# RWKV chunk inverses: holding only the two heads' 64x64 diagonal blocks, and multiplying within them

## The chip, the core and the metric

One Trainium2 chip, of which the kernel uses one core. The metric is the device time of one execution in microseconds, the median of several runs. The core's engines work side by side, each through its own list of instructions in order: TensorE (PE in the profile, with its weight loads as PEld) multiplies matrices into PSUM, VectorE (DVE) and ScalarE (ACT) work elementwise and copy out of PSUM, GpSimd (POOL) works elementwise from SBUF, and SyncE (SP) issues the transfers. SBUF and PSUM have 128 partitions, the rows of a tile. A product `mm(out, lhsT, rhs)` loads lhsT as the weights and streams the columns of rhs past them; its form in the profile is rows\*columns of the weights, then what is streamed. "128\*64 128x64" is a product over 128 partitions with 64 output rows and 64 streamed columns. Each float32 product of this kernel appears as two instructions.

## The reference

Two layers of a hybrid backbone over 1024 latent and 256 context tokens with 1024 features, ending in an RMS norm. The first layer runs RWKV-7 time mixing beside Mamba-2, the second mLSTM beside attention. The part in question is the RWKV-7 scan, 8 heads of 64 features, in both directions of time:

```python
def step(S, inp):
    r_t, k_t, v_t, w_t, a_t, kk_t = inp
    Skk = jnp.einsum('dbhvk,dbhk->dbhv', S, kk_t)
    S = S * w_t[..., None, :] - Skk[..., :, None] * (kk_t * a_t)[..., None, :] + v_t[..., :, None] * k_t[..., None, :]
    return S, jnp.einsum('dbhvk,dbhk->dbhv', S, r_t)

xs = (dir_stack(r), dir_split(k_dir), dir_stack(v), dir_split(decay), dir_split(a), dir_stack(kk))
S_fin, y = lax.scan(step, S0, xs)
```

The kernel does not scan token by token. It takes 64 tokens at a time; within such a chunk the dependence of each token on the earlier ones is a triangular 64x64 system, and its inverse is applied to the whole chunk at once.

## The kernel before

The whole first layer but RWKV comes first, then a stage with RWKV alone and part of the first layer's output product (`oa` in the profile) between, then the rest. The RWKV stage works on pairs of heads: partitions 0 to 63 belong to one head, 64 to 127 to the other (`H[0]`, `H[1]`). Four such pairs (`ct`) go as two streams (`st` 0 and 1), each over two pairs one after the other. For each pair there are ten units (`gi`) of `NG` = 2 chunks in each direction, so `NJ` = 4 chunks of 64 tokens for each head. `lockstep` advances the two streams in turn; within a stream `pace` advances the next unit (`rwkv_unit`, which needs no state) beside the chain of the present one (`rwkv_chain`, which carries the state). 20 units a stream, 40 in all. The framework's scheduler then orders the instructions of each engine from this; in this stage no order is fixed by hand.

`rwkv_unit` computes decays and products elementwise on DVE and ACT (`P`, `E2`, `sg`, `AR`, `KB`), multiplies KB with AR on TensorE (64 rows, 128 columns) and masks the result into `MN`. From it it forms `MT`, the identity less the strictly triangular part, for each of the 4 chunks. Then `TT` becomes the transposed inverse by doubling: it starts from `MT` masked to pairs of tokens (`m1`), and for block sizes b = 2, 4, 8, 16, 32 (a level each)

- `px` = MT times Tm on TensorE, masked by DVE into `Xs` (L769);
- `pz` = TT times Xs, copied by ACT into the next `Tm` (L775), not at the last level;
- `pt` = Xs times TT, copied by ACT back into `TT` (L779).

PSUM tiles of these are `rec` (two buffers a stream, `rec0` and `rec1`). `MT` and `TT` hold, for each chunk, a 128x128 matrix with the two heads' 64x64 blocks on the diagonal and zeros elsewhere, put there once by a memset at the start; `Tm` and `Xs` hold the two heads' 64x64 blocks one above the other. `halves` issues for each chunk a product for the one head and one for the other, each over all 128 rows with 64 output columns; the zeros take the other head's rows out.

`rwkv_chain` runs for each chunk, both directions at a time, through PSUM tiles `ch`: `pw` = MN times the state and values `SV`; `pu` = TT times w (`ch<-w,TT`); the next state `pS` from SV, the identity (`mk`) and `KT`; the output `py` from MN, RZ and SV. All of its products have 128 rows and 64 columns.

Of the kernel before, what the change touches and what calls it, by code (L numbers as in the profile page):

```python
# [8 lines left out]
F32 = mybir.dt.float32  # L9
# [15 lines left out]
NG = 2  # L25
# [22 lines left out]
def _masks():  # L48
    parts = []
    o = 0  # L50

    def put(name, a):
        nonlocal o
        a = np.asarray(a, np.float32).reshape(128, -1)
        _MK[name] = (o, a.shape[1])
        parts.append(a)
        o += a.shape[1]

    put("id", np.eye(128))
    put("ones", np.ones((128, 128)))  # L60
    r = np.arange(128)
    hh = (r[:, None] // 64 == r[None, :] // 64)
    put("bd1", hh)
    put("triu", r[:, None] <= r[None, :])
    put("slt", r[:, None] < r[None, :])
    for d in range(2):
        ok = (r[:, None] <= r[None, :]) if d == 0 else (r[:, None] >= r[None, :])
        put(f"mb{d}", np.where(ok, 0.0, -1e30))
    put("end", np.zeros((128, 0)))
    i = r % 64  # L70
    mp, m1, lv = [], [], {b: [] for b in (1, 2, 4, 8, 16, 32)}
    for d in range(2):
        bef = (i[:, None] < np.arange(64)[None]) if d == 0 else (i[:, None] > np.arange(64)[None])
        inc = bef | (i[:, None] == np.arange(64)[None])
        beffull = (i[:, None] < i[None, :]) if d == 0 else (i[:, None] > i[None, :])
        mp += [np.concatenate([bef, inc], 1)] * NG
        m1.append((hh & beffull & (i[:, None] // 2 == i[None] // 2)) | np.eye(128, dtype=bool))
        for b in lv:
            c = np.arange(64)[None]
            lv[b].append(~inc & (i[:, None] // (2 * b) == c // (2 * b)) & (i[:, None] // b != c // b) | (i[:, None] == c))  # L80
    put("mP", np.concatenate(mp, 1))
    put("m1", np.concatenate(m1, 1))
    put("id2", i[:, None] == np.arange(64)[None])
    for b in lv:
        put(f"l{b}", np.concatenate(lv[b], 1))
    return np.ascontiguousarray(np.concatenate(parts, 1))
# [64 lines left out]
class K:  # L151
# [401 lines left out]
    def rwkv_setup(s, rp):  # L553
        nc = s.nc
        s.rp = rp
        s.mk2 = rp.tile([128, MASKS.shape[1] - NMK], F32, name="mk2")
        s.load(s.mk2, s.I["masks"][:, NMK:])
        s.w2 = rp.tile([128, 512], F32, name="w2")
        s.a2 = rp.tile([128, 512], F32, name="a2")
        s.load(s.w2, s.I["w2"])  # L560
        s.load(s.a2, s.I["a2"])
        s.smask = rp.tile([128, 2, NG, 64], F32, name="smask")
        nc.vector.memset(s.smask, 1.0)
        for d in range(2):
            nc.vector.memset(s.smask[:, d, :, 63 * d:63 * d + 1], 0.0)
        s.rc = rp.tile([128, 28], F32, name="rc")
        nc.vector.tensor_scalar_mul(s.rc[:, 0:16], s.p("w0", 0, 16), 0.5)
        ka = s.p("k_a", 0, 4)
        nc.vector.tensor_scalar_mul(s.rc[:, 16:20], ka, 0.5)
        nc.vector.tensor_scalar(s.rc[:, 20:24], ka, -0.5, 1.0, ALU.mult, ALU.add)  # L570
        nc.vector.tensor_scalar(s.rc[:, 24:28], ka, -1.0, 2.0, ALU.mult, ALU.add)
        s.tt, s.wa, s.rz, s.mt = {}, {}, {}, {}
        for st in range(2):
            for i in range(2):
                s.tt[st, i] = rp.tile([128, 2 * NG, 128], F32, name=f"TT{st}{i}")
                s.wa[st, i] = rp.tile([128, 2, 2, 64 * NG], F32, name=f"wa{st}{i}")
                s.rz[st, i] = rp.tile([128, 2 * NG, 2, 64], F32, name=f"RZ{st}{i}")
                nc.gpsimd.memset(s.tt[st, i], 0.0)
                nc.gpsimd.memset(s.wa[st, i], 0.0)
                nc.gpsimd.memset(s.rz[st, i], 0.0)  # L580
            s.mt[st] = rp.tile([128, 2 * NG, 128], F32, name=f"MT{st}")
            nc.gpsimd.memset(s.mt[st], 0.0)
        s.RX = {}
        s.tn = [0, 0]
        s.kk_d = [s.dram("kkd", (128, NT)) for _ in range(4)]
        s.bv_d = [s.dram("bvd", (128, NT)) for _ in range(4)]
        s.vt_d = [s.dram("vtd", (128, 20, 64)) for _ in range(4)]
# [60 lines left out]
    def rwkv_unit(s, st, ct, gi):  # L648

        nc, rp = s.nc, s.rp  # L650
# [6 lines left out]
        H = [slice(0, 64), slice(64, 128)]  # L657
# [81 lines left out]

        ident = s.m("id")  # L740
        for h in range(2):
            nc.vector.scalar_tensor_tensor(MT[H[h], :, H[h]], MN[H[h], :, 0, h], -1.0,
                                           ident[H[h], H[h]].unsqueeze(1).to_broadcast([64, NJ, 64]), ALU.mult, ALU.add)
        KT = tl("KT", [2, 64], 2)
        pk = [rec(64) for h in range(2)]
# [13 lines left out]

        Tm = tl("Tm", [64], 2)  # L760
        px = rec(64)
        halves(lambda j, Q: s.mm(px[Q, j], MT[:, j, Q], s.m("id2")))
        nc.vector.tensor_mul(dj(Tm), dj(px), bj("l1"))  # L763
        yield
        for b in (2, 4, 8, 16, 32):
            px = rec(64)
            halves(lambda j, Q: s.mm(px[Q, j], MT[:, j, Q], Tm[:, j]))
            Xs = tl("Xs", [64])
            nc.vector.tensor_mul(dj(Xs), dj(px), bj(f"l{b}"))  # L769
            yield  # L770
            if b < 32:
                pz = rec(64)
                halves(lambda j, Q: s.mm(pz[Q, j], TT[:, j, Q], Xs[:, j]))
                Tm = tl("Tm", [64], 2)
                nc.scalar.copy(Tm, pz)  # L775
            pt = rec(64)
            halves(lambda j, Q: s.mm(pt[Q, j], Xs[:, j], TT[:, j, Q]))
            for h in range(2):
                nc.scalar.copy(TT[H[h], :, H[h]], pt[H[h]])  # L779
            yield  # L780
        X["u", gi] = {"E2": E2, "MN": MN, "KT": KT, "SV": SV, "TT": TT, "RZ": RZ}

    def rwkv_chain(s, st, ct, gi):
        nc, rp = s.nc, s.rp
        X = s.RX[ct]
        H = [slice(0, 64), slice(64, 128)]
        U = X["u", gi]
        SV, TT, MN, KT, E2, RZ = (U[k] for k in ("SV", "TT", "MN", "KT", "E2", "RZ"))
        if gi == 0:
            X["y"] = rp.tile([128, 2, 20, 64], F32, tag=f"y{st}", name=s.name("y"))  # L790
        J = [(n, 2 * NG - 1 - n) for n in range(NG)]

        def both(t, n):
            return t[:, J[n][0]:J[n][1] + 1:J[n][1] - J[n][0]]

        if gi == 0:
            for h in range(2):
                nc.vector.memset(both(SV, 0)[H[h], :, 0, h], 0.0)

        def ch():  # L800
            return s.psum(f"ch{st}", (128, 2, 64))

        E = E2.rearrange("p j l -> p (j l)")
        ident = s.m("id")
        for n in range(NG):
            js = J[n]
            pw = ch()
            for d, j in enumerate(js):
                for h in range(2):
                    s.mm(pw[H[h], d], MN[:, j, 0, h], SV[:, j, 0, h])  # L810
            w = rp.tile([128, 2, 64], F32, tag=f"w{st}", name=s.name("w"))
            nc.scalar.mul(w, pw, -1.0)
            yield
            pu = ch()
            for d, j in enumerate(js):
                for h in range(2):
                    s.mm(pu[H[h], d], TT[:, j, H[h]], w[:, d])
            nc.vector.tensor_copy(both(SV, n)[H[0], :, 1, 0], pu[H[0]])
            nc.scalar.copy(both(SV, n)[H[1], :, 1, 1], pu[H[1]])
            yield  # L820
            if not (gi == s.NU - 1 and n == NG - 1):
                pS = ch()
                for d, j in enumerate(js):
                    for h in range(2):
                        s.mm(pS[H[h], d], ident[:, H[h]], SV[:, j, 0, h], True, False)
                    for h in range(2):
                        s.mm(pS[H[h], d], KT[:, j, h], SV[:, j, 1, h], False, True)
                nx = SV if n < NG - 1 else X["sv", gi + 1]
                e0 = 64 * js[0] + 63
                e1 = 64 * js[1]  # L830
                PL = E[:, e0:e1 + 1:e1 - e0].unsqueeze(2).to_broadcast([128, 2, 64])
                for h in range(2):
                    nc.vector.tensor_mul(both(nx, (n + 1) % NG)[H[h], :, 0, h], pS[H[h]], PL[H[h]])
                yield
            py = ch()
            for d, j in enumerate(js):
                for h in range(2):
                    s.mm(py[H[h], d], MN[:, j, 1, h], SV[:, j, 1, h], True, False)
                for h in range(2):
                    s.mm(py[H[h], d], RZ[:, j, h], SV[:, j, 0, h], False, True)  # L840
            nc.scalar.copy(X["y"][:, :, NG * gi + n], py)
            yield
# [1204 lines left out]
```

## Time and profile before

| | |
|---|---|
| median of 3 runs | 3814.51 us |
| lowest, highest | 3805.86, 3820.41 us |
| the profiled execution's own time | 3798.59 us |
| its span | 3796.8 us |
| its mean granted TensorE clock | 0.934 |
| busy: PE, PEld | 3400.6 us (90%), 2723.1 us (72%) |
| busy: DVE, ACT, POOL | 2253.9 us (59%), 1575.3 us (41%), 1087.7 us (29%) |

The shares are means over the whole span, of which the RWKV stage takes about a quarter (some 914 of 3796.8 us). A matmul's length in the profile runs to its modelled end, while the next one starts much earlier; how fast TensorE really goes is read from the distance between two starts. The profile's page has a chain of waits as well, but it follows the end of the program back through attention only and does not reach this stage, so the stage is read by its own stretches.

### The profile page before, as it was taken

How to read it: one execution, taken by the hardware profiler on the slowest of the kernel's cores; microseconds unless marked ns; L12 is line 12 of the kernel's file. 1: busy time of each engine (PE TensorE's matmuls, PEld its weight loads, DVE VectorE, ACT ScalarE, POOL GpSimd, SP SyncE). 2: the span in 40 equal slices, each digit the busy share in tenths (PEclk: the TensorE clock that was granted, in tenths of full speed). 3: DMA queues.
4: the chain of work that ended last, by engine and by line, in shares of the span. 5: the costliest groups of instructions: out<-in, count | busy, mean ns of one | idle time of the engine just before them, and what ended most of it. 6: DMA issues, size and time to landing. Idle time of an engine off the chain costs nothing. (4 is left out here: it accounts for less than half of the span.)

```text
span 3796.8 us, 74389 instructions
## 1 busy us (share of the span) xinstructions
PE 3400.6 (90%) x29178; PEld 2723.1 (72%) x29178; DVE 2253.9 (59%) x4173; ACT 1575.3 (41%) x3419; POOL 1087.7 (29%) x1037
## 2 busy tenths in 40 slices
PE   7999998886898898789869899999999788999978
PEld 3687876673577777677757798788888566666757
DVE  3576587773566667677557705433444488677645
ACT  3232233333535656555533322322232225666751
POOL 0112266553322221121102212112222255444330
PEclk9999998997899988799879999999999899999989
DMA  6526454436543222221132322654554451000023
GB/s 237 180 75 199 138 173 149 156 124 182 153 124 99 63 69 65 82 56 47 32 111 100 124 91 85 190 180 138 161 160 147 146 157 54 23 23 22 19 81 111
DMA packets 394278, 429.65 MB, mean 113 GB/s; under 512 B 81376, under 2 KB 317760, under 8 KB 391368
## 3 DMA queue, kind: packets, MB, share of 16 engines
q1 hardware_dynamic: 393928, 424.90, 35.7%
q8 instruction: 230, 3.77, 0.4%
q14 instruction: 120, 0.98, 0.1%
HBM read 306.69 MB, written 118.05 MB: 112 GB/s over the span
## 5 line engine op out<-in xcount | busy, mean ns | idle before, releaser
L212 PE MATMUL mm<-hh,wh 128*128 128x512 f32 (+1 forms) x1640 | 634.8, 387 | 0.0
L212 PE MATMUL mm<-hh,wl 128*128 128x512 f32 (+1 forms) x1640 | 610.4, 372 | 0.9 <-POOL wl L359 0.9
L212 PE MATMUL mm<-hl,wh 128*128 128x512 f32 (+1 forms) x1640 | 610.6, 372 | 0.0
L359 POOL TENSOR_TENSOR wl<-wr,wh 128x1024 fp32r<-128x1024 f32 x99 | 248.3, 2512 | 543.1 <-ACT wh L358 520.9
L212 PEld LDWEIGHTS mm<-hh,wh 128*128 128x128 f32 x1640 | 315.0, 192 | 67.8 <-issue 12.7
L212 PEld LDWEIGHTS mm<-hl,wh 128*128 128x128 f32 x1640 | 314.6, 192 | 61.4 <-issue 10.6
L212 PEld LDWEIGHTS mm<-hh,wl 128*128 128x128 f32 x1640 | 313.9, 191 | 59.5 <-issue 3.4
L1792 POOL TENSOR_SCALAR aP<-aP,adn,one 128x1280 f32<-128x1280 f32 x128 | 191.9, 1499 | 283.5 <-DVE adn L1791 160.5
L212 PE MATMUL mm<-wh,hh 128*128 128x256 f32 x736 | 217.1, 295 | 0.0
L1785 DVE TENSOR_REDUCE amx<-sc 128x1 f32<-128x1024 f32 x128 | 156.1, 1219 | 101.6 <-PE sc L212 101.4
L212 PE MATMUL mm<-wl,hh 128*128 128x256 f32 x736 | 208.6, 283 | 3.4 <-POOL wl L359 2.5
L212 PE MATMUL mm<-wh,hl 128*128 128x256 f32 x736 | 208.2, 283 | 0.0
L215 PE MATMUL tp<-mk,aP 128*128 128x128 f32 x1280 | 181.9, 279 | 4.7 <-ACT aPT L1800 4.7
L1800 ACT COPY aPT<-tp 128x512 f32<-128x512 f32 x256 | 145.4, 587 | 83.6 <-PE tp L215 81.9
L215 PEld LDWEIGHTS tp<-mk,aP 128*128 128x128 f32 x1280 | 143.5, 142 | 35.7 <-issue 21.2
L212 PE MATMUL pv<-aPT,aV 128*64 128x256 f32 x1280 | 168.8, 395 | 0.0
L358 ACT CAST wh<-wr 128x1024 fp32r<-128x1024 f32 x99 | 103.2, 1045 | 152.7 <-PE mm L212 123.9
L779 ACT COPY TT<-rec 64x256 f32<-64x256 f32 x400 | 146.4, 366 | 37.6 <-PE rec L212 19.4
L212 PE MATMUL sc<-akT,aqs 128*128 128x512 f32 x512 | 153.9, 423 | 1.7 <-DVE aqs L1770 1.1
L1073 POOL TENSOR_SCALAR sel<-mk,mdfd,mdt 128x128 f32<-128x128 f32 x160 | 128.7, 818 | 76.7 <-DVE E L1097 57.7
L212 PE MATMUL rec<-Tm,MT 128*64 128x64 f32 x3200 | 138.4, 229 | 13.5 <-DVE Tm L763 6.6
L212 PE MATMUL oa<-wh,yh 128*128 128x512 f32 x288 | 127.3, 442 | 22.3 <-DVE o L1224 10.9
(425 smaller groups left out, 8136.8 us busy)
## 6 DMA issues: line engine op xcount, KB each, us to landing
wr<-in_wcd SPq DMA_DIRECT2D x60, 512.0 KB, 5.7
adaw<-in_ada SPq DMA_DIRECT2D x48, 512.0 KB, 5.2
R<-rowd SPq DMA_DIRECT2D x20, 1024.0 KB, 5.3
wr<-in_wab SPq DMA_DIRECT2D x38, 512.0 KB, 4.0
yr<-y SPq DMA_DIRECT2D x36, 512.0 KB, 4.2
xt<-xtok SPq DMA_DIRECT2D x20, 512.0 KB, 5.3
SV<-vtd SPq DMA_DIRECT2D x320, 32.0 KB, 2.2
lva<-lv SPq DMA_DIRECT2D x19, 514.0 KB, 5.0
```

Of the source, the lines that this page charges most:

```text
L212: return s.nc.tensor.matmul(out, lhsT, rhs, start=start, stop=stop)
L215: return s.nc.tensor.transpose(out, in_, ident)
L358: nc.scalar.copy(hi, raw)
L359: nc.gpsimd.tensor_sub(lo, raw, hi.bitcast(F32))
L779: nc.scalar.copy(TT[H[h], :, H[h]], pt[H[h]])
L1073: nc.gpsimd.tensor_scalar(sel[:, h], s.m("slt"), s.dfd[:, o:o + 1], dtb[:, h:h + 1], ALU.mult, ALU.add)
L1785: nc.vector.tensor_reduce(mx[:, 1:2], ps, AX.X, ALU.max)
L1792: nc.gpsimd.tensor_scalar(P, P, dn[:, 3:4], s.one, ALU.mult, ALU.mult)
L1800: copy(out, pp.rearrange("p (a b) q -> p a (b q)", a=out.shape[1]))
```

## The change

`MT` and `TT` become [128, 4, 64]: the two heads' blocks one above the other, without zeros and without memsets. Each product of the inverse, and `pu` in the chain, takes the 64 rows of its own head for both operands, so it becomes 64 rows by 64 columns. The mask `m1` has 64 columns for each direction instead of 128. ACT's copy into TT becomes one over 128 partitions in place of two over 64. DVE's operation for the first TT has half the columns. The chain's other products keep their 128 rows.

```diff
-        beffull = (i[:, None] < i[None, :]) if d == 0 else (i[:, None] > i[None, :])
...
-        m1.append((hh & beffull & (i[:, None] // 2 == i[None] // 2)) | np.eye(128, dtype=bool))
+        c = np.arange(64)[None]
+        m1.append(bef & (i[:, None] // 2 == c // 2) | (i[:, None] == c))
...
-                s.tt[st, i] = rp.tile([128, 2 * NG, 128], F32, name=f"TT{st}{i}")
+                s.tt[st, i] = rp.tile([128, 2 * NG, 64], F32, name=f"TT{st}{i}")
...
-                nc.gpsimd.memset(s.tt[st, i], 0.0)
...
-            s.mt[st] = rp.tile([128, 2 * NG, 128], F32, name=f"MT{st}")
-            nc.gpsimd.memset(s.mt[st], 0.0)
+            s.mt[st] = rp.tile([128, 2 * NG, 64], F32, name=f"MT{st}")
...
-            nc.vector.scalar_tensor_tensor(MT[H[h], :, H[h]], MN[H[h], :, 0, h], -1.0,
+            nc.vector.scalar_tensor_tensor(MT[H[h]], MN[H[h], :, 0, h], -1.0,
...
-        halves(lambda j, Q: s.mm(px[Q, j], MT[:, j, Q], s.m("id2")))
+        halves(lambda j, Q: s.mm(px[Q, j], MT[Q, j], s.m("id2")[Q]))
...
-            halves(lambda j, Q: s.mm(px[Q, j], MT[:, j, Q], Tm[:, j]))
+            halves(lambda j, Q: s.mm(px[Q, j], MT[Q, j], Tm[Q, j]))
...
-                halves(lambda j, Q: s.mm(pz[Q, j], TT[:, j, Q], Xs[:, j]))
+                halves(lambda j, Q: s.mm(pz[Q, j], TT[Q, j], Xs[Q, j]))
...
-            halves(lambda j, Q: s.mm(pt[Q, j], Xs[:, j], TT[:, j, Q]))
-            for h in range(2):
-                nc.scalar.copy(TT[H[h], :, H[h]], pt[H[h]])
+            halves(lambda j, Q: s.mm(pt[Q, j], Xs[Q, j], TT[Q, j]))
+            nc.scalar.copy(TT, pt)
...
-                    s.mm(pu[H[h], d], TT[:, j, H[h]], w[:, d])
+                    s.mm(pu[H[h], d], TT[H[h], j], w[H[h], d])
```

TensorE's order in the levels of a late round, before. In a row the part before the arrow is the output, then the operands, then the output's rows and columns and how many follow each other; the numbers belong to buffers.

```order
L212 MATMUL rec_3473_19597<-Tm_19545,MT_6803 64x64 x8
L212 MATMUL rec_3475_19608<-Tm_19574,MT_6817 64x64 x8
L212 MATMUL ch_3480_19641<-SV_18483,mk 64x64
L212 MATMUL rec_3477_19619<-Xs_19606,TT_6797 64x64 x8
L212 MATMUL rec_3479_19630<-TT_6797,Xs_19606 64x64 x8
L212 MATMUL ch_3480_19641<-SV_18483,mk 64x64
L212 MATMUL ch_3480_19641<-SV_18483,KT_18629 64x64 x2
```

The same place on TensorE in the changed kernel:

```order
L211 MATMUL rec_3473_19422<-Tm_19372,MT_6801 64x64 x8
L211 MATMUL rec_3475_19433<-Tm_19400,MT_6812 64x64 x8
L211 MATMUL ch_3480_19465<-SV_18324,mk 64x64
L211 MATMUL rec_3477_19444<-Xs_19431,TT_6796 64x64 x8
L211 MATMUL rec_3479_19455<-TT_6796,Xs_19431 64x64 x8
L211 MATMUL ch_3480_19465<-SV_18324,mk 64x64
L211 MATMUL ch_3480_19465<-SV_18324,KT_18468 64x64 x2
```

The products stand in the same order. What the rows don't say is that every row had 128\*64 weights before, while now the rows with MT or TT have 64\*64 weights and those with SV still 128\*64.

ACT's order at the same place, before:

```order
L775 COPY Tm_19545<-rec_3465_19536 128x256
L779 COPY TT_6797<-rec_3467_19547 64x4x64 x2
L775 COPY Tm_19574<-rec_3469_19565 128x256
L779 COPY TT_6805<-rec_3471_19576 64x4x64 x2
L841 COPY y_16342<-ch_3472_19587 128x2x64
```

And in the changed kernel:

```order
L772 COPY Tm_19372<-rec_3465_19363 128x256
L775 COPY TT_6796<-rec_3467_19374 128x256
L772 COPY Tm_19400<-rec_3469_19391 128x256
L775 COPY TT_6802<-rec_3471_19402 128x256
L837 COPY y_16217<-ch_3472_19412 128x2x64
```

Each pair of copies into TT is one now; nothing else has moved here. Elsewhere in the stage the scheduler has shifted a few rows against each other.

More of the change, by code (lines that the diff above doesn't have):

```diff
@@ L74, in _masks @@
         inc = bef | (i[:, None] == np.arange(64)[None])
-        beffull = (i[:, None] < i[None, :]) if d == 0 else (i[:, None] > i[None, :])
         mp += [np.concatenate([bef, inc], 1)] * NG
-        m1.append((hh & beffull & (i[:, None] // 2 == i[None] // 2)) | np.eye(128, dtype=bool))
+        c = np.arange(64)[None]
+        m1.append(bef & (i[:, None] // 2 == c // 2) | (i[:, None] == c))
         for b in lv:
-            c = np.arange(64)[None]
             lv[b].append(~inc & (i[:, None] // (2 * b) == c // (2 * b)) & (i[:, None] // b != c // b) | (i[:, None] == c))
```

## The prediction

> **What bounds the kernel now.** I read the page's span first, then the busy time by stretches, to find the stage that the change touches and what limits it there, then the groups of that stage, then TensorE's matmuls one after another.
>
> ```profile
> span 3796.8 us, 74389 instructions
> ```
>
> The profiled execution has a span of 3796.8 us and a time of 3798.59 us. The median of the three runs is 3814.51 us (3805.86 to 3820.41), so the profile lies 16 us below it; I make the sum as a difference and add it to the median. Where the touched work lies (duration ns min/median/max, first and last start us):
>
> ```profile
> L578 POOL MEMSET TT<- x4: 523/523/523, 860.0 to 864.7; 128x512 f32 x4
> L212 PE MATMUL rec<-mk,MT x640: 222/222/369, 973.1 to 1863.5; 128*64 128x64 f32 x160
> L779 ACT COPY TT<-rec x400: 348/367/373, 981.4 to 1883.1; 64x256 f32<-64x256 f32 x134
> ```
>
> The RWKV stage's inverses run from 973 us to 1883 us: 40 units, two streams side by side, so 20 rounds in some 914 us.
>
> Busy time by stretches; columns are PE, weight loads, DVE, ACT, POOL with their counts, then the granted clock, DMA share and GB/s. The first three rows are 100 us pieces of the stage, the last two the two halves of one late round:
>
> ```profile
> 1200.00:1300.00 100.00, 92.25 (x1966) 79.24 (x1963) 69.48 (x165) 59.96 (x174) 17.18 (x23) 0.93 0.27 74
> 1500.00:1600.00 100.00, 77.12 (x1138) 62.15 (x1140) 66.25 (x135) 57.45 (x138) 18.79 (x26) 0.73 0.30 86
> 1700.00:1800.00 100.00, 92.05 (x2182) 80.73 (x2182) 71.82 (x174) 60.31 (x186) 18.93 (x24) 1.00 0.20 50
> 1705.00:1722.00 17.00, 16.00 (x470) 15.12 (x464) 8.34 (x20) 10.52 (x32) 2.17 (x3) 1.00 0.12 29
> 1722.00:1739.00 17.00, 15.35 (x287) 12.43 (x286) 16.27 (x40) 10.03 (x33) 4.64 (x6) 1.00 0.28 72
> ```
>
> A round alternates. In 1705 to 1722 (the levels of both streams' inverses) TensorE starts 470 instructions and DVE is half idle. In 1722 to 1739 (decays, KB, MN, MT of the next units) DVE is busy 16.27 of 17 us and TensorE starts only 287. So the first half belongs to TensorE and the second to DVE, and what the change adds to TensorE is paid in the first half, what it takes from DVE is gained in the second.
>
> TensorE's timeline (start, length, form rows\*columns, count). A merged row's step is its length less one matmul's 0.22 us, over its count less one:
>
> ```profile
> 1720.35 0.63 PE L212 MATMUL rec<-TT,Xs 128*64 128x64 f32 x15
> 1720.87 0.30 PE L212 MATMUL ch<-SV,RZ 128*64 128x64 f32 x3
> 1721.10 1.16 PE L212 MATMUL rec<-AR,KB 64*128 64x128 f32 x14
> 1722.18 0.45 PE L212 MATMUL ch<-w,TT 128*64 128x64 f32 x8
> 1722.57 0.48 PE L212 MATMUL mm<-wa,a 128*128 128x256 f32 x1
> ```
>
> Fifteen 128\*64 instructions: (0.63 - 0.22) / 14 = 0.029 us a step. At 470 instructions that is 13.6 of the 17 us, so TensorE steps without a pause for 80% of that half and waits for a result in the rest. The other thing to see is the change of form. The last 128\*64 matmul starts at 1720.87 + 0.30 - 0.22 = 1720.95, the first 64\*128 one at 1721.10: 0.15 us instead of 0.029. Again: the last ch<-w,TT starts at 1722.18 + 0.45 - 0.22 = 1722.41, and the 128\*128 matmul behind it at 1722.57: 0.16. A change of form costs about 0.12 us over a step. I counted 515 of them down TensorE's order in the stage before.
>
> **The change part by part.** The groups it touches (line, engine, out<-in, shapes, count | busy us, mean ns | idle before):
>
> ```profile
> L779 ACT COPY TT<-rec 64x256 f32<-64x256 f32 x400 | 146.4, 366 | 37.6 <-PE rec L212 19.4 <-PE ch L212 0.7
> L775 ACT COPY Tm<-rec 128x256 f32<-128x256 f32 x160 | 59.5, 372 | 103.1 <-PE rec L212 101.2
> L752 DVE TENSOR_TENSOR TT<-MT,mk 128x512 f32<-128x512 f32 x40 | 27.3, 682 | 0.2
> L769 DVE TENSOR_TENSOR Xs<-rec,mk 128x256 f32<-128x256 f32 x200 | 83.6, 422 | 81.0 <-PE rec L212 78.4
> L742 DVE SCALAR_TENSOR_TENSOR MT<-MN,mk 64x256 f32<-64x256 f32 x80 | 36.6, 457 | 1.3
> L578 POOL MEMSET TT<- 128x512 f32 x4 | 2.1, 523 | 0.0
> L582 POOL MEMSET MT<- 128x512 f32 x2 | 1.0, 524 | 0.0
> L212 PE MATMUL rec<-Tm,MT 128*64 128x64 f32 x3200 | 138.4, 229 | 13.5 <-DVE Tm L763 6.6 <-ACT Tm L775 5.7 <-ACT KT L750 0.6
> L212 PEld LDWEIGHTS rec<-Tm,MT 128*64 128x64 f32 x3200 | 118.5, 141 | 31.9 <-issue 10.4 <-ACT Tm L775 9.4 <-ACT TT L779 3.2
> L212 PE MATMUL rec<-TT,Xs 128*64 128x64 f32 x3200 | 136.6, 224 | 3.0 <-DVE Xs L769 2.5
> L212 PE MATMUL rec<-Xs,TT 128*64 128x64 f32 x2560 | 114.7, 229 | 9.9 <-DVE Xs L769 7.3
> L212 PE MATMUL rec<-mk,MT 128*64 128x64 f32 x640 | 34.9, 252 | 4.0 <-DVE MT L742 2.8 <-ACT KT L750 1.0
> L212 PE MATMUL ch<-w,TT 128*64 128x64 f32 x640 | 44.0, 239 | 3.8 <-ACT w L812 3.8
> ```
>
> *The products.* 3200 + 3200 + 2560 + 640 + 640 = 10,240 instructions (two for each f32 product) go from 128 rows to 64; their number, their 64 output columns and 64 streamed columns stay. No 64\*64 matmul stands in this trace. The two nearest rows are the 128\*64 one, 0.029 us a step where two halves of 64 columns take turns, and the 64\*128 one: rec<-AR,KB, where two halves of 64 rows take turns, (1.16 - 0.27) / 13 = 0.068 us with its slow start for 128 streamed columns, so about 0.034 for 64. The upper end would be +0.005 x 10,240 = +51 us, and a lower one of the same size is as far. I take 0.029, no difference, because the halves still take turns and 64 columns still stream.
>
> The Trainium skill, "TensorE: Matmul & The Clock Gate", Part 3 on packing small matmuls, says that a weight load overlaps running matmuls only when its row group differs. This trace does not agree: the loads above have a mean of 0.141 us, all in one row group, and still a step takes 0.029. What the sum would be by the rule is the fourth rival below.
>
> *The changes of form.* The other products of the chain (MN, KT, RZ, the identity) keep 128 rows, and they lie between the levels. Down the new order I count 968 changes instead of 515; of these 455 are between 64\*64 and 128\*64, where before both sides were one form. About 20 of each round's 23 lie in TensorE's half: 20 rounds x 20 x 0.12 us = 48 us. TensorE steps without a pause for 80% of that half, and a change that falls in a wait is covered by it: 0.8 x 48 = 38, I take +39 us. Ends: nothing, if all fall in waits; 455 x 0.16 = 73 us if each costs a whole gap and none is covered.
>
> *TT's copy.* 400 copies of 366 ns become 200 of 128x256, for which the Tm copy of that shape shows 372: 146.4 - 74.4 = 72 us less on ACT. In TensorE's half ACT is busy 10.52 of 17 us and waits 101.2 us in all for those very products, so most is cover. Who waited for TT (us, times):
>
> ```profile
> PEld rec L212: 8.0, 21
> PEld ch L212: 2.6, 8
> ```
>
> That is 10.6 us; with one copy in place of two, half of it: -5 us. Ends: 0, and 21 + 8 waits x 0.366 = -11 us, doubled to -22 for the Tm, SV and y copies that queue behind TT on ACT.
>
> *TT's first value.* 40 operations go from 128x512 (682) to 128x256 (422, by L769): 40 x 0.26 = -10 us, in the half where DVE is 16.27 of 17 us busy, so I count all. Ends: -10 and 0. MT's two operations (L742) keep their shape: 0.
>
> *Setup.* Six memsets, 3.1 us of POOL, and 128 columns of the masks' load go. They stand at 860 us, the first product of the inverse at 973, over 100 us later and behind the preparation of the first heads; 0, at most -3.
>
> Sum: 39 - 5 - 10 = +24, so 3798.6 + 24 = 3823 us for a profiled run like this one and 3814.5 + 24 = 3839 us for the median, 0.6% slower. A difference under 0.5%, 19 us, can't be told from none by a measurement of this kernel.
>
> **Rivals.** *The new changes are covered or cheap.* The chain's products are what the order puts in where a level waits for Xs or TT, so a change may stand where TensorE would have waited. For it: the waits of the table. Against it: they come to 13.5, 3.0, 9.9, 4.0 and 3.8 us over the whole stage, less than the 48 us to hide. If a third is left, 16 - 15 = +1: 3815 us.
>
> *Faster.* ACT is the lock: the shorter queue lets Tm, SV and y through, -22, with DVE's -10 and no cost on TensorE: 3782 us. It decides when a change between the two 64-column forms costs under 0.04 us on the path (15 / 400). Against it: every change of form shown above costs about 0.12, whichever forms.
>
> *The two halves no longer run together.* Both write one rec tile, upper half and lower, in the same bank; the 64\*128 products that alternate rows in this trace write two different tiles, so no row shows the case. If they took turns the step would be that of the pair, 0.058: 10,240 x 0.029 x 0.8 = +238 on top of 24, 4077 us. The Trainium skill, "TensorEngine Tiling (Array Packing)", Restrictions and Gotchas, states that different row tiles can't access one PSUM bank at the same time; the 128\*64 rows above share a bank without harm, but those are column halves. I give it little, since the two halves touch different partitions.
>
> *The loads come out from under.* If half of each step is now an exposed load, two row groups would free it: 10,240 x 0.0145 x 0.8 = -119, with the +24 about 3720 us. The Trainium skill's rule on row groups, above, would give this. The equal steps with hidden loads speak against it.
>
> *The clock.* If the gate counts how much of the array works, the levels at half the rows look as thin as the emptiest stretch, 0.73 granted against 0.93 and 1.00. For TensorE's half of the stage, 457 us: 457 x (0.97 / 0.73 - 1) = +150 with 0.97 between the other two rows, 3989 us. That stretch has fewer instructions (1138 against 1966 and 2182), not narrower ones, so nothing shows it.
>
> **How the numbers follow.** Forecast 0.58, its own range 3822 to 3885 us: below by half of the changes covered, above by every gap whole with neither gain (3814.5 + 73 = 3888). Covered 0.21, 3795 to 3825. Faster by ACT 0.07. Halves in turn 0.06. Loads freed 0.03. Clock 0.05. The range reaches over the first three, down to 3782 and up past 3888 to 3890, which leaves the last three and some edge, 0.17. Slower by over 0.5% (above 3833.6): 0.46 of the forecast's 0.58, both expensive cases, together 0.57. Faster (below 3795.4): 0.07 + 0.03 + 0.02 of the covered = 0.12. The same: the remaining 0.31.
>
> **What would show it.** Right: the levels' rows read 64\*64 with steps of 0.029, a first 64\*64 matmul about 0.15 us behind a 128\*64 one, TensorE's half of a late round 18.5 to 20 us instead of 17, L779's line with x200 at 372 ns, TT's first value at about 0.42. Wrong: gaps of 0.03 to 0.06 at the changes, steps of 0.058, a granted clock below 0.9 in 1650 to 1850 us, or a DVE half that shortens by more than 0.5 us a round.

## The result, and the profile after

The changed kernel takes 3835.22 us (median of five runs, 3833.78 to 3840.99) against 3814.51 us before. The ratio of the runs is 1.0072, with a 95% interval of 1.0055 to 1.009: slower by 0.7%, or 27 us of 3814.5. A second comparison of the same kernel on another occasion gave 1.0081 (1.0065 to 1.0098). The forecast was 3839 us. Among all executions of this study one, of the kernel with DVE's operation done three times, took 8099 us and is left out of its ratio.

The page of the changed kernel begins:

```profile
span 3839.2 us, 74212 instructions
```

The profiled pair differs by 42 us because the profiled execution of before lay 16 us under its own median and that of the changed kernel 6 us over; sizes below are therefore taken from the ratios, and the traces are used for places and reasons.

The groups that the change touched, in the changed kernel (line, engine, out<-in, shapes, count | busy us, mean ns | idle before). Line numbers have moved by one to four: TT's copy is L775 now, its first value L749.

```profile
L211 PE MATMUL rec<-Tm,MT 64*64 64x64 f32 x3200 | 138.2, 231 | 8.2 <-DVE Tm L760 6.2 <-ACT E L704 0.9 <-ACT sg L706 0.6
L211 PEld LDWEIGHTS rec<-Tm,MT 64*64 64x64 f32 x3200 | 115.8, 142 | 29.3 <-issue 8.9 <-ACT TT L775 3.4 <-DVE Tm L760 2.3
L211 PE MATMUL rec<-Xs,TT 64*64 64x64 f32 x2560 | 115.2, 231 | 3.3 <-DVE Xs L766 2.9
L775 ACT COPY TT<-rec 128x256 f32<-128x256 f32 x200 | 74.5, 373 | 53.8 <-PE rec L211 38.3 <-PE ch L211 0.4
L772 ACT COPY Tm<-rec 128x256 f32<-128x256 f32 x160 | 59.5, 372 | 148.7 <-PE rec L211 145.1 <-DVE SV L829 2.4
L749 DVE TENSOR_TENSOR TT<-MT,mk 128x256 f32<-128x256 f32 x40 | 17.7, 442 | 0.3
```

ACT's copies into TT fell from 146.4 to 74.5 us, as the count and the shape said, and DVE's first value from 682 to 442 ns. A product over 64 rows takes as long as one over 128 (231 against 229 ns, the load 142 against 141). But ACT's Tm copy now sits idle for 145.1 us until TensorE's products, where it was 101.2: ACT was freed, and waits for TensorE.

TensorE's timeline in the levels of a late round (start, length, form, count):

```profile
1733.59 0.40 PE L211 MATMUL rec<-mk,MT 64*64 64x64 f32 x8
1733.82 0.63 PE L211 MATMUL rec<-Tm,MT 64*64 64x64 f32 x16
1734.38 0.33 PE L211 MATMUL ch<-SV,MN 128*64 128x64 f32 x2
1734.64 0.68 PE L211 MATMUL rec<-Tm,MT 64*64 64x64 f32 x16
1735.25 0.27 PE L211 MATMUL ch<-SV,MN 128*64 128x64 f32 x1
```

Within the second row the step is (0.63 - 0.22) / 15 = 0.027 us, much as in the 128\*64 form. The last of its matmuls starts at 1733.82 + 0.63 - 0.22 = 1734.23 and the first of the chain's MN products at 1734.38: 0.15 us. The second of those starts at 1734.38 + 0.33 - 0.22 = 1734.49, and the next 64\*64 one at 1734.64: 0.15 again. One small chain product between two blocks of the inverse costs a gap on each side.

The gap is not all of it. The second row of sixteen, behind a change, is 0.68 us long, while the first, which follows products of its own form, has 0.63. Single starts show why. The matmuls mostly start in pairs, 3 to 7 ns apart, and the next pair follows 52 to 55 ns later; 0.029 us is the mean of the two. Behind a change the first pair comes 0.15 us late, and the second pair another 0.10 us behind it instead of 0.052. Over the changed kernel's stage, from the last matmul before a change between 64\*64 and 128\*64 to the fifth behind it are 0.314 to 0.317 us (median, 415 places), and without a change 0.169, also where the tile changes from rec to ch and the form doesn't. So a change costs about 0.145 us over ordinary steps, not the 0.12 read from the first gap alone.

The two halves of a late round in the changed kernel, and then before, cut in both at the same places: from the second unit's first rec<-mk,MT to the next rec<-AR,KB (the levels), and from there to the second unit's next rec<-mk,MT (columns as in the prediction: PE, weight loads, DVE, ACT, POOL with counts, granted clock, DMA share, GB/s).

```profile
1733.20:1749.90 16.70, 16.69 (x447) 15.24 (x443) 6.84 (x19) 7.65 (x23) 1.56 (x2) 0.99 0.09 21
1749.90:1770.50 20.60, 19.10 (x280) 15.60 (x279) 15.30 (x36) 9.04 (x30) 4.62 (x6) 0.85 0.25 63
```

```profile
1737.50:1753.00 15.50, 14.47 (x446) 13.64 (x442) 8.67 (x21) 10.11 (x31) 2.40 (x3) 1.00 0.12 29
1753.00:1771.00 18.00, 16.38 (x293) 13.39 (x292) 15.42 (x39) 10.00 (x33) 3.91 (x5) 1.00 0.26 65
```

The levels went from 15.5 to 16.7 us, and TensorE is now busy in all of them (16.69 of 16.70). The other half went from 18.0 to 20.6 us, although DVE has a shorter operation there: DVE's work is 15.30 us instead of 15.42, and it now idles 5.3 of 20.6 us. TensorE is busy 19.10 of that half. So both halves are TensorE's now. Part of the 2.6 us goes with the granted clock, 0.85 in that half; in the kernel with two copies (below), at a clock of 1.00 throughout, the levels take 16.3 and 17.2 us and the other half 18.9 and 19.7 in two rounds, so both still lengthen, by about 1.3 us each.

The levels also show what covers a change. Before, 6 starts in 1737.5 to 1753.0 come over 0.12 us behind the one before without a change of form, 2.4 us in all: TensorE waits there, and part of each wait lies within the modelled 0.22 us of the matmul before it, so that the busy time doesn't show it. In the changed kernel's levels there is no such start left, but 21 changes where there was none. At 0.145 us they are 3.0 us; less the waits that went, 2.4 - 6 x 0.052 = 2.1, that gives +0.9, and the levels are 1.2 us longer.

Counted from the starts of TensorE's matmuls in whole late rounds (1719.5 to 1753.0 before, 1749.9 to 1787.6 after), there are some 20 changes of form before and 49 after. Thirty of the 49 are between 64\*64 and 128\*64; from start to start they take 4.7 us, 0.156 each; at 0.145 us over ordinary steps, thirty cost 4.4 us, of which the waits above cover a part. The round is 4.2 us longer. The granted clock also differs in that round, 0.91 against 1.00, which the experiments take up.

### The profile page after: what moved, and what is told of

The parts are those of the page before. It is cut to its first block, busy times and chain, and to the rows that moved or that the text cites. A ratio compares the mean times of both kernels' runs of the same rounds, so it can differ in the third digit from the quotient of the medians.

```text
span 3839.2 us, 74212 instructions
## 1 busy us (share of the span) xinstructions
PE 3465.0 (90%) x29178; PEld 2766.3 (72%) x29178; DVE 2239.0 (58%) x4173; ACT 1508.5 (39%) x3219; POOL 1082.8 (28%) x1031
## 5 line engine op out<-in xcount | busy, mean ns | idle before, releaser
L211 PE MATMUL rec<-Tm,MT 64*64 64x64 f32 x3200 | 138.2, 231 | 8.2 <-DVE Tm L760 6.2
L211 PEld LDWEIGHTS mm<-wl,hh 128*128 128x128 f32 x736 | 141.3, 192 | 3.2 <-POOL wl L358 1.9
```

What stands on the lines that cost most here:

```text
L211: return s.nc.tensor.matmul(out, lhsT, rhs, start=start, stop=stop)
```

## The experiments

Theory: TensorE pays about 0.12 us for each change between 64\*64 and 128\*64, and ACT and DVE give some 15 us back. Rival "rows": the products over 64 rows cost, by a lower granted clock. Rival "placement": the narrow tiles or the shifted order cost, not the products. Ratios are to the kernel before, measured beside it; microseconds are (ratio - 1) x 3814.5. Changes of form are counted down TensorE's order in the stage. The traces, from the first product of the inverse to the last of the chain, hold 2 to 9% more added changes (492 for 455, 646 for 632), and 10,240 and 1248 instructions over 64 rows where the expectations say 10,224 and 1224; the prices below would be that much lower.

**The narrow tiles with 128 rows.** All of the change but the rows of the products:

```diff
-        halves(lambda j, Q: s.mm(px[Q, j], MT[Q, j], s.m("id2")[Q]))
+        halves(lambda j, Q: s.mm(px[Q, j], MT[:, j], s.m("id2")))
...
-            halves(lambda j, Q: s.mm(pt[Q, j], Xs[Q, j], TT[Q, j]))
+            halves(lambda j, Q: s.mm(pt[Q, j], Xs[:, j], TT[:, j]))
```

(and so for px in the levels, pz and pu). The heads are mixed in these products, so this kernel doesn't compute the reference; it is there for its time alone.

> The changed kernel's narrow MT and TT, its one copy by ACT and its half-width first TT, but every product over all 128 rows (128*64 weights), so that the two heads are mixed; the masks m1 and l2 to l32 are scaled by 0.25 to keep the values small. 511 changes of form in the stage, as before (515). Theory (each change of form costs about 0.12 us, DVE and ACT give back 15 us): 3814.5 - 15 = 3800 us, ratio 0.996, and a granted clock in 1650 to 1850 us as before, near 1.0. Rival 'rows' (the changes are covered, the products over 64 rows lower the granted clock): also about 3800, with the clock near 1.0. Rival 'placement' (narrow tiles or the shifted order cost the time, not the products): 3830 to 3840, ratio above 1.004. Rival 'ACT is the lock': 3782, ratio 0.991.

Measured: 0.9949 (0.9933 to 0.9965), -19 us. Placement falls: the narrow tiles alone make the kernel faster. From here to the changed kernel, 457 changes more, is 1.0072 - 0.9949 = 0.0123 (0.0099 to 0.0147), 47 us (38 to 56), or 0.10 us for each change.

**The wide tiles with 64 rows.** The other half of the change alone:

```diff
-                halves(lambda j, Q: s.mm(pz[Q, j], TT[:, j, Q], Xs[:, j]))
+                halves(lambda j, Q: s.mm(pz[Q, j], TT[Q, j, Q], Xs[Q, j]))
```

(and so for the other products).

> The kernel before with its wide MT and TT, its zeros, memsets and two copies, but every product of the inverse and pu over the 64 rows of its own head (64*64 weights). 970 changes of form, 455 more than before; 10,224 instructions over 64 rows. Theory: the +39 us of the changes without the gains, 3853 us, ratio 1.010. Rival 'rows': the same 3853, but with half-clock stretches in 1650 to 1850 us. Rival 'placement': 3815, ratio 1.000.

Measured: 1.0098 (1.0073 to 1.0123), +37 us for 455 changes, 0.08 each; expected +39. Together the two halves of the change give -19 + 37 = +18 us, against 27 measured, within their intervals.

**Many changes, few 64-row products.** In the kernel before, the chain's identity and RZ products have zeros in the other head's rows, so they can be cut to 64 rows alone:

```diff
-                        s.mm(pS[H[h], d], ident[:, H[h]], SV[:, j, 0, h], True, False)
+                        s.mm(pS[H[h], d], ident[H[h], H[h]], SV[H[h], j, 0, h], True, False)
...
-                    s.mm(py[H[h], d], RZ[:, j, h], SV[:, j, 0, h], False, True)
+                    s.mm(py[H[h], d], RZ[H[h], j, h], SV[H[h], j, 0, h], False, True)
```

> The kernel before, only two of the chain's products over the 64 rows of their own head: the identity times SV and RZ times SV (the zeros in the other rows made them so already). 1147 changes of form, 632 more than before and more than the changed kernel's 968, but only 1224 instructions over 64 rows instead of 10,224. Theory: 632 x 0.12 x 0.8 = +61 us, 3875 us, ratio 1.016 (1.010 if half are covered). Rival 'rows': 1224 / 10,224 of 39 us = +5, 3819, ratio 1.001, granted clock in 1650 to 1850 us near 1.0. Rival 'placement': 3815, ratio 1.000.

Measured: 1.0227 (1.0203 to 1.025), +87 us: more than three times the changed kernel's loss, with an eighth of its 64-row products. That decides against "rows". The price, 87 / 632 = 0.137 us (0.123 to 0.151), is above the expected 0.8 x 0.12, and above 0.12 itself; of the 0.145 us that a change takes with its second step, about nine tenths are paid by this sum. In the late rounds at a clock of 1.00 it is less: 37.2 us a round instead of 33.5 with 38 more changes, 0.097 each. Twenty such rounds make 74 of the 87 us; where the rest lies was not read. TensorE's timeline of this kernel, one chain step between two products of the inverse:

```profile
1807.98 0.33 PE L212 MATMUL ch<-SV,mk 64*64 64x64 f32 x2
1808.24 0.34 PE L212 MATMUL ch<-SV,KT 128*64 128x64 f32 x4
1808.50 0.33 PE L212 MATMUL ch<-SV,mk 64*64 64x64 f32 x4
1808.77 0.34 PE L212 MATMUL ch<-SV,KT 128*64 128x64 f32 x4
```

From the last matmul of a row (start + length - 0.22) to the first of the next are 1808.09 to 1808.24, 1808.36 to 1808.50 and 1808.61 to 1808.77: 0.14 to 0.16 us each time, where the four matmuls of a row lie within 0.12.

**The same products, fewer changes.** Of each two chunks the second takes its two parts the other way round, so that parts of one form meet:

```diff
-                for d, j in enumerate(js):
-                    for h in range(2):
-                        s.mm(pS[H[h], d], ident[H[h], H[h]], SV[H[h], j, 0, h], True, False)
-                    for h in range(2):
-                        s.mm(pS[H[h], d], KT[:, j, h], SV[:, j, 1, h], False, True)
+                for d, j in enumerate(js):
+                    for a in ((0, 1), (1, 0))[d]:
+                        for h in range(2):
+                            if a == 0:
+                                s.mm(pS[H[h], d], ident[H[h], H[h]], SV[H[h], j, 0, h], d == 0, d == 1)
+                            else:
+                                s.mm(pS[H[h], d], KT[:, j, h], SV[:, j, 1, h], d == 1, d == 0)
```

(and so for py).

> The kernel with the chain's identity and RZ products over 64 rows, once more, with the same products in another order: of each two chunks the second takes its two parts the other way round, so that parts of one form meet. The same 1224 instructions over 64 rows, but 1009 changes of form instead of 1147, 494 more than before instead of 632. Theory (the changes themselves cost): 494 x 0.137 = +68 us, ratio 1.018; with 0.12 each, 1.0155. Rival (the 64-row products, or splitting a sum between two forms, cost, whatever the number of changes): 1.0225 as for 632.

Measured: 1.0167 (1.0142 to 1.0191), +64 us or 0.129 for each of 494 changes; 23 us (10 to 36) less than with 632. The time follows the number of changes while the products stay the same. Its trace can't be set against the other round by round: it is of the slowest of its executions (3878 us), at a clock of 0.875 in five late rounds of 40.9 us, while the rounds of the kernel with 632 changes take 37.2 at 1.00. So the 0.129 may hold some half-clock time too.

**Only px over 64 rows.** The kernel before, with `MT[Q, j, Q], Tm[Q, j]` for `MT[:, j, Q], Tm[:, j]` (and so for the first px).

> The kernel before, only px (MT times Tm) over the 64 rows of its own head; pz, pt and pu keep 128 rows. 791 changes of form, 276 more than before; 3840 instructions over 64 rows. Theory, with the price that the runs so far give for a change of form (0.08 us from the wide tiles with 64 rows, 0.10 from the changed kernel against the narrow tiles with 128 rows): +23 to +28 us, ratio 1.006 to 1.0075; with 0.137 us, the price in the chain, +38, ratio 1.010. Rival 'rows' (what costs is the number of instructions over 64 rows): 3840 / 10,224 of the wide tiles' +37 = +14, ratio 1.0035.

Measured: 1.0054 (1.0034 to 1.0074), +21 us for 276 changes, 0.075 each. The interval holds "rows" too (1.0035), so this run alone tells nothing apart; it stands as a third dose.

**ACT's copies.** The changed kernel, and the narrow tiles with 128 rows, each with two copies again:

```diff
-            nc.scalar.copy(TT, pt)
+            for h in range(2):
+                nc.scalar.copy(TT[H[h]], pt[H[h]])
```

> The changed kernel with ACT's copy into TT as two copies over 64 partitions again (64x256 each, 400 in all). Theory: ACT's term alone, +5 us on the changed kernel's 3835, 3840 us, ratio to before 1.0085. Rival 'ACT is the lock': +22, 3857 us, ratio 1.011 to 1.013. If the copies are hidden: 3835, ratio 1.007.

> The narrow tiles with products over 128 rows (heads mixed, masks scaled by 0.25), but ACT's copy into TT as two over 64 partitions again, so that of the change only DVE's narrower first TT (and the layout) is left. 513 changes of form. The narrow tiles with one copy ran at 0.9949 of before. Theory of the prediction (ACT's term 5 us): 0.996. If ACT's term is the larger one, because DVE's counted only by half where it was tripled: 0.9985 to 1.000.

Measured: 1.008 (1.0057 to 1.0103) with 64 rows, 0.9981 (0.9965 to 0.9998) with 128 rows. With 128 rows the single copy is worth 0.0032 (0.0009 to 0.0055), 12 us (3 to 21). With 64 rows it is 3 us (-8 to 14) against the first comparison of the changed kernel and nothing against the second. That is what the Tm copy's longer wait for TensorE shows: the time that ACT saves is spent waiting. The 0.9981 that is left is DVE's first value and the layout: -7 us (-13 to -1).

**DVE's first value, three times over.** The line `nc.vector.tensor_mul(dj(TT), dj(MT), bj("m1"))` of the changed kernel stands there three times.

> The changed kernel with DVE's operation for the first TT (128x256) done three times over, 80 operations of 0.442 us or 35 us more on DVE, in the half of a round that is DVE's. 933 changes of form against 968. Theory of the prediction (there every microsecond of DVE counts): +35 us on the changed kernel, ratio to before 1.0165. Rival (DVE's half has slack, and the gain on the narrow tiles was ACT's): 1.007 to 1.010.

Measured: 1.0115 (1.0095 to 1.0136), +16 us (6 to 27) on the changed kernel for 35 us of DVE. Neither expectation: about half counts (its order has 35 changes of form less, worth some 3 us by the prices above, so it may be a little more). DVE's half has slack, but not for everything.

**DVE's first value shared with GpSimd**, in the kernel before:

```diff
-        nc.vector.tensor_mul(dj(TT), dj(MT), bj("m1"))
+        for h, e in ((0, nc.vector), (1, nc.gpsimd)):
+            e.tensor_mul(dj(TT)[H[h], :, :, H[h]], dj(MT)[H[h], :, :, H[h]], bj("m1")[H[h], :, :, H[h]])
```

> The kernel before with its products over 128 rows, but the first TT only on the two diagonal blocks: head 0's 64x256 by DVE, head 1's by GpSimd, in place of one 128x512 operation of 682 ns by DVE. 512 changes of form, as before. Theory: DVE gets (682 - 457) x 40 = 9 us back in its half, 3805 us, ratio 0.9975; if DVE's term was sized too low by the narrow tiles' -19 us against -15: 0.996. Rival (DVE's half has slack): 1.000. Rival (GpSimd comes too late with its half, or holds DVE up): above 1.003.

Measured: 1.0002 (0.999 to 1.0015). The two groups, by line:

```profile
L753 POOL TENSOR_TENSOR TT<-MT,mk 64x256 f32<-64x256 f32 x40 | 37.9, 947 | 143.1 <-DVE MT L742 130.2 <-DMA SV<-vtd 8.0 <-DMA r<-urk 2.6
...
L753 DVE TENSOR_TENSOR TT<-MT,mk 64x256 f32<-64x256 f32 x40 | 17.2, 431 | 1.2
```

DVE got 682 - 431 = 251 ns back 40 times, 10 us, and nothing came of it: TT's first value was there only when GpSimd's half, 947 ns long, was done. Whether that delay or the slack ate the gain, this run doesn't tell.

**The changed kernel once more**, for the clock.

> The changed kernel unaltered, for a second profile beside a second comparison. Its first profile shows a granted clock of 0.93 in 1640 to 1880 us, where before shows 0.99 and the changed kernel with two copies, over the same 64 rows, 0.99. Theory (the changes of form alone; the clock there differs from one profile to the next): ratio 1.007, and a clock anywhere from 0.93 to 0.99 with late rounds of 36 to 38 us. Rival 'rows' (products over 64 rows lower the clock): 0.93 again, late rounds of 38 us again.

Measured: 1.0081 (1.0065 to 1.0098). The late rounds, by the granted clock in the third column from the right: before, the changed kernel's first and second profile, the one with two copies (64 rows), and the regrouped chain (nearly all products over 128 rows).

```profile
1640.00:1880.00 240.00, 218.25 (x5186) 192.10 (x5181) 166.61 (x396) 142.52 (x432) 40.00 (x51) 0.99 0.16 41
```

```profile
1640.00:1880.00 240.00, 230.43 (x4552) 196.69 (x4552) 149.88 (x378) 105.48 (x330) 41.49 (x54) 0.93 0.17 43
```

```profile
1640.00:1880.00 240.00, 227.84 (x4584) 194.28 (x4581) 152.76 (x387) 107.40 (x337) 43.57 (x57) 0.96 0.18 45
```

```profile
1640.00:1880.00 240.00, 228.50 (x4755) 194.62 (x4756) 161.36 (x402) 132.95 (x410) 44.97 (x58) 0.99 0.18 45
```

```profile
1640.00:1880.00 240.00, 228.30 (x4223) 191.11 (x4221) 145.63 (x353) 119.77 (x367) 38.71 (x50) 0.88 0.16 41
```

The clock is 0.99 with 10,240 instructions over 64 rows in one kernel and 0.88 with 1248 in another, so it doesn't follow the rows. Where it is low the rounds are longer: in the kernel with two copies five late rounds (from one unit's first rec<-mk,MT to that of the unit after the next, from 1682.7 us on) take 35.8 to 36.3 us at a clock of 1.00. In the changed kernel five from 1677.9 us on take 36.9 to 39.3, the shortest of them at 1.00; in its second profile three at 1.00 take 36.1 to 36.9. Before it is 33.5. So some 2.6 to 3.4 of the 4.6 us that such a round has lost on average come with the changes of form at full clock, and the rest goes with half-clock stretches. What brings these on was not isolated.

**TensorE in the written order.** The RWKV stage put into `manual_schedule` for TensorE, so that its instructions stand in the order of the program; pieces of chain and inverse stay longer together.

> The changed kernel with TensorE's order in the RWKV stage as the program is written, instead of the scheduler's: chain and inverse stay together in longer pieces, 668 changes of form against 968. Theory: 300 fewer changes x 0.1 us = -30 us on the changed kernel, 3805 us, ratio to before 0.999, if TensorE waits no more than before. Rival (in the written order TensorE stands before products whose inputs come late): those waits outweigh it, ratio above 1.01.

Measured: 1.0457 (1.0442 to 1.0472). Fewer changes and yet far slower, as the rival said:

```profile
1640.00:1880.00 240.00, 192.77 (x3812) 164.57 (x3812) 130.78 (x314) 98.16 (x287) 37.39 (x48) 0.81 0.18 49
L211 PE MATMUL rec<-Xs,TT 64*64 64x64 f32 x2560 | 118.5, 237 | 34.0 <-DVE Xs L766 32.1
```

In the late rounds TensorE is busy for 192.77 of 240 us instead of 230.43, and before the products of Xs with TT alone it waits 32.1 us for DVE, where it was 2.9. The scheduler's mixing of chain and inverse, which makes the changes of form, is what fills these waits.

**The copies on two engines.** To have ACT's gain without changes of form, in the kernel before:

```diff
-            for h in range(2):
-                nc.scalar.copy(TT[H[h], :, H[h]], pt[H[h]])
+            nc.scalar.copy(TT[H[0], :, H[0]], pt[H[0]])
+            nc.vector.tensor_copy(TT[H[1], :, H[1]], pt[H[1]])
```

> The kernel before with products over 128 rows; of the two copies into TT head 0's stays on ACT and head 1's goes to DVE, which is half idle in TensorE's half of a round. 515 changes of form, as before. ACT has 200 x 366 ns = 73 us less, as with one copy over 128 partitions, DVE some 80 us more. Theory: ACT's term as the narrow tiles show it with 128 rows (0.9949 against 0.9981, 12 us) is to be had without changes of form: 0.997. Rival (Xs, MT and SV now queue behind the copies on DVE): 1.003 to 1.01. If both cancel: 1.000.

Measured: 1.0054 (1.0034 to 1.0073). Its groups show why:

```profile
L212 PE MATMUL rec<-Xs,TT 128*64 128x64 f32 x2560 | 115.4, 230 | 24.0 <-DVE Xs L769 21.4 <-ACT a L692 0.7 <-ACT w L812 0.5
...
L779 DVE COPY TT<-rec 64x256 f32<-64x256 f32 x200 | 85.2, 428 | 79.5 <-ACT TT L778 75.6
```

DVE's copy sat idle for 75.6 us until ACT's copy of the other head was done: the two ran one after another, not side by side. The next Xs queued behind on DVE, and TensorE waited 21.4 us for it instead of 7.3. No kernel of this study that computes the reference was faster than the one before.

## Why the prediction was right

The forecast, 3839 us and slower, came out (3835), by the mechanism that it named: changes of form between 64\*64 and 128\*64, for the most part paid. The closeness of the number is in part luck, as its terms show one by one:

*The step over 64 rows*: forecast no different. It is 0.027 to 0.029 us, so the "halves in turn" (0.058) and the "loads freed" (half of 0.029) both fall. On the first, the Trainium skill, "TensorEngine Tiling (Array Packing)", Restrictions and Gotchas, says that different row tiles can't access one PSUM bank at the same time; in this trace two heads' row tiles write disjoint partitions of one rec tile in turn, and the step doesn't lengthen.

*The price of a change*: forecast 0.12 us over a step. The gaps of 0.15 us are there in both directions, but the prediction took the start behind the gap for the end of the matter; with the longer second step it is 0.145 us, a fifth more. The Trainium skill, "TensorEngine Tiling (Array Packing)", Tiling Modes, says that switching the mode drains TensorE, without a price. The trace fits that: a second step of 0.10 us stands behind a change, and also behind a wait of 0.16 us and more without a change (median before); whether TensorE is empty at a change no run shows.

*How many are paid*: forecast 20 of 23 a round in one half, 80% of them paid, +39 us in all. The size held (37 us with wide tiles, 38 with two copies, 47 with one, intervals of about 10 either way), but its reasoning did not. There are 20 in the levels, as forecast, but about two fifths of their cost is paid there (1.2 of 3.0 us), where I had looked for 1.5 to 3 us more. The waits that I had counted, 34 us over the stage, are too few to cover so much, because the idle column leaves out what lies within a matmul's modelled 0.22 us: in the levels above TensorE is idle for 1.0 us, where its late starts lose 2.1. And a late round has thirty new changes, not 23: ten lie in the half that I had called DVE's, and it pays as well. The misreading was to take a DVE busy 16.27 of 17 us for the only lock, in a stretch where TensorE, at 15.35 of 17, had little slack to give either. A price too low, a share too high and a half left out came to the right sum.

*ACT's copy*: forecast -5 us, measured -12 (-21 to -3) with 128 rows and nothing that can be told with 64. *DVE's first value*: forecast -10 with all of it counted; measured -7 (-13 to -1) with 128 rows, and when it was tripled only about half of it counted. "I count all" was too much, for the same reason as above. *Setup*: not tried by itself.

With the terms as measured the sum is +47 - 12 - 7 = +28 us, against +24 forecast. That it meets the +27 found shows nothing more, since the three are differences along one chain of runs and add up to it by construction; the halves of the change measured apart give +18, within their intervals. All three terms were off by some microseconds, the changes upwards and ACT's copy downwards, and cancelled.

Two of the prediction's own figures don't follow from it: half of the changes covered gives 3819 us (19.5 - 15), not 3822, and its range ends at 3885 where the same sentence reckons 3888. Neither moves the forecast. And 0.5% was not the least that can be told: the interval of the first comparison is 0.0018 either way.

*The rivals*: "covered or cheap" asked for a third of the cost to be left. In the levels two fifths are left, so it was near the truth there. Over the whole time the inverse pays half to seven tenths of 0.145 us a change and the chain more, so it falls on the total. "ACT is the lock" asked for a change below 0.04 us. "The clock" asked for 0.73 in the levels; they show 0.99 and the stage's late rounds 0.93 to 0.96, and the kernel with two copies shows that 64 rows do not need to lower it. The sign that I had set for it, below 0.9 in 1650 to 1850 us, did not come up, though half-clock stretches that I had not allowed for did.

What stays open: why a change costs 0.13 us in the chain and 0.075 to 0.10 in the inverse. On TensorE both take the same 0.145 us. In late rounds at a clock of 1.00 the round pays 0.097 for each of the chain's, and 0.078 and 0.060 with the wide tiles and with px alone (32 and 18 more changes, rounds of 36.0 and 34.6 us). That waits cover a part is shown for the levels; why they cover less of the chain's is not. And what brings on the half-clock stretches in the late rounds.

## What to carry to other kernels

Count the changes of form down TensorE's order, not the array that a product uses: cutting products from 128 to 64 rows saved TensorE nothing (the step stayed 0.027 to 0.029 us), and each change to and from the neighbours that kept 128 rows cost about 0.1 us of the kernel's time. Measure such a change over several matmuls behind it: here the second step was longer too. If one product of a mixed stretch is made smaller, make its neighbours the same form or leave it. A busy engine in a stretch isn't its only lock: if a second one is nearly as busy there, what you add to the first may count by about half (16 of 35 us here), and what you add to the second is paid as well.

## What the hardware showed that I had not expected

- A product over 64 rows and one over 128 differ in nothing but form: 231 against 229 ns a matmul, 142 against 141 ns a load, one step.
- Breaking a sum up between two forms was the dearest edit of the study for its size: some 1200 instructions cut to 64 rows cost 87 us, 0.137 us for each of the 632 changes that they made.
- A change of form delays two steps, 0.15 us and then 0.10 instead of 0.052, about 0.145 us in all; a change of tile at the same form delays none.
- The granted clock in one and the same 240 us of the span was 0.93 and 0.96 in two profiles of one kernel, and between 0.88 and 0.99 across kernels that keep TensorE busy for 228 to 230 of those 240 us.
